# Three delays in a chunk clock: when the feed-forward transposes, the recurrence's gates and the last head group's attention are issued

## The chip, the cores and the metric

The kernel runs on one core of one Trainium2 chip. The metric is the time of one execution on the device in microseconds, as the median of several runs. A core has a matrix engine (PE, whose weight loads the profile lists apart as PEld), a vector engine (DVE), an activation engine (ACT), GpSimd (POOL) and a sync engine (SP); each has an instruction queue of its own and works it off in order. Here SP issues nearly all loads from HBM.

## The reference

Two transformer blocks over 256 tokens of width 2048, in float32. The first has a gated linear recurrence and a windowed attention side by side, then a feed-forward layer; the second has gated linear attention with decay, then a feed-forward layer.

```python
u = causal_depthwise_conv(u, conv_w[l], conv_b[l])
r = sigmoid(einsum(uh, wa) + ba); i = sigmoid(einsum(uh, wx) + bx)      # the recurrence's gates
...                                                                     # a linear scan over tokens
y_attn = sliding_window_attention(q, k, v, sinks[l])                    # 16 heads, 4 key/value heads
merged = gate_lru * (y_lru @ w_lru_out[l]) + gate_attn * (y_attn @ w_attn_out[l])
x = x + g1 * (merged @ w_o[l])
gate, up = jnp.split(h2 @ w_ffn_in[l], 2, axis=-1)
x = x + g2 * ((jax.nn.silu(gate) * up) @ w_ffn_out[l])                  # hidden width 5632
...                                                                     # the second block ends alike:
x = x + swiglu(rms_norm_2(x, norm_g[i, 1]), ffn_w_gu[i], ffn_w_down[i])
```

## The kernel before

**Chunks.** All large products run over *chunks*: a block of 512x512 weights, 1 MB, loaded by SP into a buffer `raw` (three of them). `split` casts each half of a chunk to a rounded part `hi` on ACT (line 173) and takes the remainder `lo` on DVE (line 175); there are three `hi` and three `lo` half-chunk buffers. `accumulate` then issues three matmuls per product (high by high, high by low, low by high): 48 matmuls of 256 columns per chunk, called narrow here (lines 197, 199, 201), or, where the output has tokens on partitions, 24 of 512 columns, called wide (lines 190 to 192). `project` runs the four chunks of one group of 512 output columns into two PSUM banks (of eight).

**The chunk clock.** Everything else is written as Python generators that are interleaved with the chunks. `spawn(gen, delay)` notes a generator that is due `delay` ticks later; `pump()` adds one tick and advances each generator that is due by one step, up to its next `yield n`, which makes it due again `n` ticks later; `finish` runs one to its end at once. There is a pump after every chunk. The pump also issues `steps`: slices of a matrix-vector product, each a 512 KB load `mvw` on SP's queue and one DVE operation `mva` that adds it up (line 247).

**The scheduler.** The program written in that order is then put in its final order by a list scheduler, which moves instructions between neighbouring pieces of work and gives the weight loads, `hi` and `lo` a head start (priority offset 2000). So the place in the chunk clock decides roughly, not exactly, where an instruction stands in its engine's queue.

**The three generators.** `turned` (line 657) transposes one feed-forward group: `sg`, the product of `silu(gate)` and `up` with tokens on partitions (DVE, line 724 in the first block, 969 in the second), goes through eight 128x128 transposes on PE (`tps`, line 666) into two banks; ACT copies each to `hid` (line 668) and DVE takes the remainder (line 669). `swiglu` runs it for 6 and then 5 groups in each block, 22 in all; the `fops` products that follow read `hid`. `recur` (line 558) does the recurrence of 512 channels in steps: convolution (`uc`), the eight gate matmuls `rps` (lines 578, 579), sigmoids and exponentials, a square root, the scan. `attend` (line 366) does four heads that share one key/value head in five steps: scores of two heads; scores of the other two, maximum and exponentials; sums and normalisation; two ticks later twelve transposes `tp` (line 405) with ACT copies to `p` (line 406); one tick later the products with the values `o` (lines 410 to 413) and the output pair `ya`. The `aops` products read `ya` of head group c in chunk c, and call `finish(attn[c])` before it.

Of the kernel before, what the change touches and what calls it, by code (L numbers as in the profile page):

```python
# [49 lines left out]
def block_pair_kernel(ctx: ExitStack, tc: tile.TileContext, a: dict):  # L50
# [78 lines left out]
    def spawn(gen, delay=0):  # L129
        task = [clock[0] + delay, gen]  # L130
        tasks.append(task)
        return task
# [46 lines left out]
    def accumulate(ps, ap, src, first, last, tokens=False):  # L179

        parts = split(ap, tokens)
        for kk in range(4):
            hi, lo = parts[kk // 2]
            wk = kk % 2
            fst, lst = first and kk == 0, last and kk == 3
            if tokens:
                for t in range(2):
                    tsl = slice(t * P, (t + 1) * P)
                    xh, xl = src.hi(kk)[:, tsl], src.lo(kk)[:, tsl]
                    nc.tensor.matmul(ps[t], xh, hi[:, wk, :], start=fst, stop=False)  # L190
                    nc.tensor.matmul(ps[t], xh, lo[:, wk, :], start=False, stop=False)  # L191
                    nc.tensor.matmul(ps[t], xl, hi[:, wk, :], start=False, stop=lst)  # L192
                continue
            for f in range(4):
                wsl = slice(f * P, (f + 1) * P)
                o = ps[f // 2][:, f % 2, :]
                nc.tensor.matmul(o, hi[:, wk, wsl], src.hi(kk), start=fst and f % 2 == 0,  # L197
                                 stop=False, skip_group_check=True)
                nc.tensor.matmul(o, hi[:, wk, wsl], src.lo(kk), start=False, stop=False,  # L199
                                 skip_group_check=True)  # L200
                nc.tensor.matmul(o, lo[:, wk, wsl], src.hi(kk), start=False, stop=lst,  # L201
                                 skip_group_check=True)

    def banks(name, tokens=False):
        return [bank(name, [P, 512] if tokens else [P, 2, T]) for _ in range(2)]
# [59 lines left out]
    def ada_steps(strip, queue=nc.gpsimd):  # L265


        def done(ps):
            if strip < 4:
                cols = ((16 + 4 * strip, 0, 4), (4 * strip, 4, 4))  # L270
            else:
                cols = ((8 * strip, 0, 8),)
            for j, p, n in cols:
                nc.vector.tensor_tensor(mod[:, j:j + n], ps[:, p:p + n], v("ada_b", j, n), ALU.add)

        return matvec([a["ada_w"][strip, k] for k in range(NK)], lambda k: cact[:, k:k + 1],
                      1024, done, queue)
# [183 lines left out]
    early = {}  # L461
    ga = {}
    attn = []
    for q in range(NG):
        ahead = ada_steps(q + 1) if q < NG - 1 else []
        count = sum(len(ks) for _, ks in plan[q])
        share = -(-len(ahead) // (count - 1))
        for g, ks in plan[q]:
            tok = g == 13
            if g in held:  # L470
                if q == 0:
                    early[g] = banks(f"e{g}", tok)
                ps = early[g]
            else:
                ps = banks("part")
            for k in ks:
                if g in held:
                    accumulate(ps, a["w_in"][g, k], h[k], k == 0, k == NG - 1, tok)
                else:
                    accumulate(ps, a["w_in"][g, k], h[k], k == ks[0], k == ks[-1])  # L480
                for st in ahead[:share]:
                    st()
                if ahead and len(ahead) <= share:
                    next_h()
                ahead = ahead[share:]
                lead[0] = PREP
                if q == NG - 1 and k < ks[-1]:
                    pump()
            if g not in held:
                fresh = g not in early  # L490
                if fresh:
                    early[g] = slot(f"e{g}")
                for b, part in enumerate(halves(early[g])):
                    if fresh:
                        nc.scalar.activation(part, ps[b], AF.Copy)
                    else:
                        nc.vector.tensor_tensor(part, ps[b], part, ALU.add)
                ps = halves(early[g])
            if q == NG - 1:
                if g == 12:  # L500
                    kv["k"] = evac_bias(ps, "kT", 48)
                elif g == 13:
                    kv["v"] = slot("vn", shape=[P, 2, 512])
                    for t in range(2):
                        nc.vector.tensor_tensor(kv["v"][:, t, :], ps[t], bv, ALU.add)
                elif g < 12:
                    attn.append(spawn(attend(g - 8, early[g]), 1 + 2 * (g - 8)))
                else:
                    ga[g - 18] = evac_bias(ps, "ga", 72 + 4 * (g - 18), AF.Sigmoid,
                                           early[g])  # L510
                pump()
# [46 lines left out]
    def recur(g, ups):  # L558
        lw = slot("lw", shape=[P, 4, 2, P])
        nc.sync.dma_start(lw, a["lru_w"][g])  # L560
        u = evac_bias(ups, "u", 4 * g)
        uc = slot("uc")
        for i in range(4):
            j = 4 * g + i
            nc.scalar.activation(uc[:, i, :], u[:, i, :], AF.Identity, bias=v("conv_b", j),
                                 scale=v("conv_w", 48 + j))
            for k in (2, 1, 0):
                s = 3 - k
                nc.vector.scalar_tensor_tensor(uc[:, i, s:], u[:, i, 0:T - s],
                                               v("conv_w", 16 * k + j), uc[:, i, s:],  # L570
                                               ALU.mult, ALU.add)
        yield 1
        r = slot("r")
        ig = slot("ig")
        for i in range(4):
            j = 4 * g + i
            ps = bank("rps", [P, 2, T])
            nc.tensor.matmul(ps[:, 0, :], lw[:, i, 0, :], uc[:, i, :], start=True, stop=True)
            nc.tensor.matmul(ps[:, 1, :], lw[:, i, 1, :], uc[:, i, :], start=True, stop=True)
            nc.scalar.activation(r[:, i, :], ps[:, 0, :], AF.Sigmoid, bias=v("lru_ba", j))  # L580
            nc.scalar.activation(ig[:, i, :], ps[:, 1, :], AF.Sigmoid, bias=v("lru_bx", j))
        yield 1
        nc.vector.tensor_tensor(ig, ig, uc, ALU.mult)
        av = slot("av")
        for i in range(4):
            j = 4 * g + i
            nc.scalar.activation(av[:, i, :], r[:, i, :], AF.Exp, scale=c8[:, j:j + 1])
            nc.scalar.activation(r[:, i, :], r[:, i, :], AF.Tanh, scale=nc8[:, j:j + 1])

        aa = slot("aa")  # L590
        nc.scalar.activation(aa, av, AF.Square)
        yield 1
        nc.vector.scalar_tensor_tensor(r, aa, 1.0, r, ALU.add, ALU.mult)
        nc.scalar.activation(r, r, AF.Sqrt)
        yield 1
        nc.vector.tensor_tensor(ig, ig, r, ALU.mult)
        for i in range(4):
            nc.vector.tensor_tensor_scan(r[:, i, :], av[:, i, :], ig[:, i, :], 0.0,
                                         ALU.mult, ALU.add)
        while g not in gelu:  # L600
            yield 1
        ge = gelu.pop(g)
        nc.vector.tensor_tensor(ge, ge, r, ALU.mult)
        y_lru[g] = split_act(ge, "yr")
# [66 lines left out]
    def swiglu(w_in, w_out, gate, up, update):  # L671
        for n, half in enumerate((range(0, 6), range(6, FG))):
            hid, turns = [], []
            for j in half:
                sg = gate(j)
                pump()
                gen = turned(up(sg, j))
                hid.append(next(gen))
                turns.append(spawn(gen, 1))
                pump()  # L680
            for f in range(NG):
                chunks = chunks_of(w_out, f, list(half))
                ps = banks("fops")
                for c in range(len(chunks)):
                    finish(turns[c])
                    accumulate(ps, chunks[c], hid[c], c == 0, c == len(chunks) - 1)
                    if c < len(chunks) - 1:
                        pump()
                update(n, f, ps)
                pump()  # L690
# [383 lines left out]
```

## Time and profile before

| | |
|---|---|
| runs | median 2764.09 us of 3 (2761.22 to 2767.21) |
| the profiled execution | 2761.13 us, of which the span of its instructions is 2759.4 us |
| PE busy, weight loads busy | 98% and 90% of the span |
| DVE, ACT, POOL busy | 65%, 48%, 1% |
| moved by DMA | 602 MB, 218 GB/s on average |
| mean granted PE clock | 0.997 |

In order of time from the span's start: the front with the first norm and partial projections (to 225 us), these with attention in between (to 317), the `aops` products (to 400), the recurrence with its projections (to 640), gates and merge (to 880), feed-forward layer one (880 to 1620), linear attention (to 2050), feed-forward layer two (to the end).

A timeline row reads: start in us, busy us, engine, line and operation, output<-inputs, size, and in brackets the idle time before it with what ended it. PE is pipelined and its ends are modelled, so a row's busy time is longer than the distance to the next start; distances between starts tell what PE lost. A row of the waits reads: who waited for whom: us in total, times, longest. A row of the windows gives per engine the busy us and instructions in the stretch, then the granted PE clock (PEclk), the DMA share and GB/s.

### The profile page before, as it was taken

What the parts mean: (1) busy time and instruction counts of PE and PEld (TensorE: products, weight loads), DVE (VectorE), ACT (ScalarE), POOL (GpSimd) and SP (SyncE); (2) the same over time, 40 slices, a digit from 0 to 9 for tenths busy, and PEclk for the clock granted to TensorE, in tenths of its full rate; (3) what the DMA queues carried; (4) which work ended last, traced back from release to release, by engine and by line L of the source; (5) the groups of instructions that cost most, each with busy time, mean ns of one, the idle gap of its engine ahead of it and who ended that gap; (6) DMA issues with size and microseconds to landing.
All of it is one profiled execution on the core that took longest, in us unless ns stands there. A gap on an engine that the chain in (4) does not pass through costs nothing.

```text
span 2759.4 us, 43921 instructions
## 1 busy us (share of the span) xinstructions
PE 2691.7 (98%) x18612; PEld 2478.1 (90%) x18612; DVE 1783.9 (65%) x2000; ACT 1321.7 (48%) x1531; POOL 25.7 (1%) x52
## 2 busy tenths in 40 slices
PE   4999999999999999999999999999999999999999
PEld 4999899999999788899888999899988889988899
DVE  8888866878887865444545677866654544444544
ACT  3446537874455444434444555555554443344443
POOL 1100000000000000000000000000000000000000
PEclk9999999999999999999999999999999999999999
DMA  9984785769985876555555544445555555555554
GB/s 357 365 306 153 248 325 190 262 236 339 341 289 184 290 248 216 183 197 187 188 191 183 199 163 169 151 142 180 192 190 183 184 195 186 199 183 192 187 195 161
DMA packets 100165, 602.00 MB, mean 218 GB/s; under 512 B 11120, under 2 KB 11632, under 8 KB 40576
## 3 DMA queue, kind: packets, MB, share of 16 engines
q1 hardware_dynamic: 93056, 574.03, 59.7%
q0 software_dynamic: 6912, 25.17, 2.4%
q8 instruction: 145, 2.38, 0.3%
q14 instruction: 52, 0.43, 0.0%
HBM read 597.06 MB, written 2.10 MB: 217 GB/s over the span
## 4 chain that ended last, share of the span: by engine, by line
PE 88%; DVE 5%; DMA 3%; issue 3%; ACT 1%; POOL 0%; SPq 0%; DVEq 0%; POOLq 0%; ACTq 0%
PE fgps L191 6%; PE fgps L190 6%; PE fgps L192 6%; PE fops L197 6%; PE fops L201 6%; PE fops L199 6%; PE fups L192 5%; PE fups L190 5%; PE fups L191 5%; DMA mvw<-ada_w 3%; DVE lo L175 2%; PE part L199 1%; PE part L197 1%; PE part L201 1%; ACT hi L173 1%
## 5 line engine op out<-in xcount | busy, mean ns | idle before, releaser
L175 DVE TENSOR_TENSOR lo<-raw,hi 128x1024 fp32r<-128x1024 f32 x928 | 1134.4, 1223 | 871.2 <-ACT hi L173 869.2
L173 ACT ACTIVATE hi<-raw 128x1024 fp32r<-128x1024 f32 x928 | 983.1, 1060 | 1263.2 <-PE fups L192 274.5
L197 PE MATMUL fops<-hid,hi 128*128 128x256 f32 x1408 | 389.0, 276 | 0.0
L201 PE MATMUL fops<-hid,lo 128*128 128x256 f32 x1408 | 388.9, 276 | 0.0
L199 PE MATMUL fops<-hid,hi 128*128 128x256 f32 x1408 | 388.8, 276 | 0.0
L190 PE MATMUL fups<-hi,h 128*128 128x512 f32 x704 | 274.0, 389 | 0.0
L191 PE MATMUL fups<-lo,h 128*128 128x512 f32 x704 | 273.9, 389 | 0.0
L192 PE MATMUL fups<-hi,h 128*128 128x512 f32 x704 | 273.9, 389 | 0.0
L190 PE MATMUL fgps<-hi,h 128*128 128x512 f32 x672 | 264.7, 394 | 0.0
L199 PEld LDWEIGHTS fops<-hid,hi 128*128 128x128 f32 x1408 | 264.3, 188 | 0.0
L201 PEld LDWEIGHTS fops<-hid,lo 128*128 128x128 f32 x1408 | 264.3, 188 | 0.0
L197 PEld LDWEIGHTS fops<-hid,hi 128*128 128x128 f32 x1408 | 264.3, 188 | 0.0
L192 PE MATMUL fgps<-hi,h 128*128 128x512 f32 x672 | 263.1, 391 | 0.0
L191 PE MATMUL fgps<-lo,h 128*128 128x512 f32 x672 | 262.2, 390 | 0.0
L247 DVE SCALAR_TENSOR_TENSOR mva<-mvw,cact,mva 128x1024 f32<-128x1024 f32 x180 | 230.5, 1280 | 32.3 <-DMA mvw<-ada_w 30.4
L190 PEld LDWEIGHTS fups<-hi,h 128*128 128x128 f32 x704 | 132.1, 188 | 27.5
L192 PEld LDWEIGHTS fups<-hi,h 128*128 128x128 f32 x704 | 132.1, 188 | 27.5
L191 PEld LDWEIGHTS fups<-lo,h 128*128 128x128 f32 x704 | 132.1, 188 | 27.3
L192 PEld LDWEIGHTS fgps<-hi,h 128*128 128x128 f32 x672 | 126.3, 188 | 26.0
L191 PEld LDWEIGHTS fgps<-lo,h 128*128 128x128 f32 x672 | 126.5, 188 | 25.4
L190 PEld LDWEIGHTS fgps<-hi,h 128*128 128x128 f32 x672 | 126.5, 188 | 25.0
L197 PE MATMUL part<-h,hi 128*128 128x256 f32 x512 | 145.4, 284 | 0.0
(322 smaller groups left out, 5424.0 us busy)
## 6 DMA issues: line engine op xcount, KB each, us to landing
raw<-w_in SPq DMA_DIRECT2D x88, 1024.0 KB, 5.3
raw<-w_ffn_in SPq DMA_DIRECT2D x88, 1024.0 KB, 4.8
raw<-ffn_w_gu SPq DMA_DIRECT2D x88, 1024.0 KB, 4.8
mvw<-ada_w SPq DMA_DIRECT2D x144, 512.0 KB, 7.1
raw<-gla_w_in SPq DMA_DIRECT2D x48, 1024.0 KB, 4.8
raw<-w_ffn_out SPq DMA_DIRECT2D x44, 1024.0 KB, 4.8
raw<-ffn_w_down SPq DMA_DIRECT2D x44, 1024.0 KB, 4.9
mvw<-ada_w POOLq DMA_DIRECT2D x48, 512.0 KB, 8.5
```

What stands on the lines that cost most here:

```text
L173: nc.scalar.activation(hi, rb, AF.Copy)
L175: nc.vector.tensor_tensor(lo, rb, f32(hi), ALU.subtract)
L190: nc.tensor.matmul(ps[t], xh, hi[:, wk, :], start=fst, stop=False)
L191: nc.tensor.matmul(ps[t], xh, lo[:, wk, :], start=False, stop=False)
L192: nc.tensor.matmul(ps[t], xl, hi[:, wk, :], start=False, stop=lst)
L197: nc.tensor.matmul(o, hi[:, wk, wsl], src.hi(kk), start=fst and f % 2 == 0, stop=False, skip_group_check=True)
L199: nc.tensor.matmul(o, hi[:, wk, wsl], src.lo(kk), start=False, stop=False, skip_group_check=True)
L201: nc.tensor.matmul(o, lo[:, wk, wsl], src.hi(kk), start=False, stop=lst, skip_group_check=True)
L247: nc.vector.scalar_tensor_tensor(state["acc"], w, col(k), state["acc"], ALU.mult, ALU.add)
```

## The change

Three delays become other numbers. The transposes of a feed-forward group become due two ticks after their group instead of one. The recurrence waits two ticks between convolution and gates instead of one. The fourth head group's attention starts five ticks after it is spawned instead of seven. No instruction's work is changed.

```diff
-                    attn.append(spawn(attend(g - 8, early[g]), 1 + 2 * (g - 8)))
+                    attn.append(spawn(attend(g - 8, early[g]), (1, 3, 5, 5)[g - 8]))
...
         # in recur(), between the convolution and the gates
-        yield 1
+        yield 2
...
         # in swiglu(), after up(sg, j)
-                turns.append(spawn(gen, 1))
+                turns.append(spawn(gen, 2))
```

What that does to the queues is seen at three places. First, PE at the end of a feed-forward group (`fups` is the up product of the group, `fgps` the gate product of the next). Before:

```order
L192 MATMUL fups<-hi,h 128x512
L666 MATMUL tps<-ident,sg 128x128 x2
L190 MATMUL fgps<-hi,h 128x512
L191 MATMUL fgps<-lo,h 128x512
L666 MATMUL tps<-ident,sg 128x128 x6
L192 MATMUL fgps<-hi,h 128x512
```

And now, where between the two products 24 matmuls of the next group's first chunk stand ahead of the transposes (its first and last rows are shown):

```order
L192 MATMUL fups<-hi,h 128x512
L190 MATMUL fgps<-hi,h 128x512
...
L192 MATMUL fgps<-hi,h 128x512
L666 MATMUL tps<-ident,sg 128x128 x8
L190 MATMUL fgps<-hi,h 128x512
```

The transposes moved from both sides of the group's end to one place a chunk later, eight in a row. On ACT the copies `hid` then stand behind ten weight casts after the second `silu` instead of eight, and on DVE the remainders behind three `lo` after `sg` instead of one. At the end of a half's last group the chunk ahead of them is the first of `fops`.

Second, PE from the second head group's value products to the fourth's (`sps` are scores; s_2564 is the third head group's, s_2922 and s_2778 are the fourth's, `part` the last projections). Before:

```order
L413 MATMUL o_2749<-p_2637,vn 128x512
...
L405 MATMUL tp<-ident,s_2564 128x128 x4
L405 MATMUL tp<-ident,s_2565 128x128 x8
L368 MATMUL sps<-kT,e_632 128x128
...
L410 MATMUL o_2994<-p_2898,vn 128x512
...
L197 MATMUL aops<-ya,hi 128x256
...
L405 MATMUL tp<-ident,s_2922 128x128 x4
L405 MATMUL tp<-ident,s_2923 128x128 x6
L410 MATMUL o_3315<-p_3234,vn 128x512
L405 MATMUL tp<-ident,s_2923 128x128 x2
```

And now:

```order
L413 MATMUL o_2749<-p_2637,vn 128x512
L368 MATMUL sps<-kT,e_632 128x128
...
L405 MATMUL tp<-ident,s_2564 128x128 x4
...
L410 MATMUL o_3033<-p_2941,vn 128x512
...
L405 MATMUL tp<-ident,s_2778 128x128 x4
L405 MATMUL tp<-ident,s_2779 128x128 x8
L197 MATMUL aops<-ya,hi 128x256
...
L410 MATMUL o_3192<-p_3112,vn 128x512
```

The fourth group's first scores moved ahead of the third's transposes; its transposes moved from behind three chunks of `aops` (144 matmuls) to ahead of the first, with its value products 48 matmuls after them instead of among them. The third group's value products now stand 86 matmuls after its transposes instead of 48. On SP, five chunks of `w_attn_out` stand ahead of the next `mvw` loads where there were three, and on DVE the first `mva` of that stage stands behind all of the fourth group's softmax instead of within it. POOL's queue is the same.

Third, PE in the recurrence, within the first `gps` product. Before:

```order
L201 MATMUL gps<-h,lo 128x256
L578 MATMUL rps<-uc,lw 128x256
L579 MATMUL rps<-uc,lw 128x256
...
L199 MATMUL gps<-h,hi 128x256
L578 MATMUL rps<-uc,lw 128x256
L579 MATMUL rps<-uc,lw 128x256
...
L201 MATMUL gps<-h,lo 128x256
```

The four pairs of gate matmuls stood two and two, some ten matmuls apart, after the first chunk. Now all eight stand in one row after the second chunk:

```order
L201 MATMUL gps<-h,lo 128x256
L578 MATMUL rps<-uc,lw 128x256
L579 MATMUL rps<-uc,lw 128x256
...
L579 MATMUL rps<-uc,lw 128x256
L197 MATMUL gps<-h,hi 128x256
```

ACT's queue now holds 41 loads of activation tables where it held 47: the sigmoids of a recurrence group are no longer cut in two by its exponentials.

## The prediction

> **What bounds the kernel now.** I read the page first, then the waits, then PE's timeline at the places that the change moves.
>
> ```profile
> span 2759.4 us, 43921 instructions
> PE 2691.7 (98%) x18612; PEld 2478.1 (90%) x18612; DVE 1783.9 (65%) x2000; ACT 1321.7 (48%) x1531; POOL 25.7 (1%) x52
> PE 88%; DVE 5%; DMA 3%; issue 3%; ACT 1%; POOL 0%; SPq 0%; DVEq 0%; POOLq 0%; ACTq 0%
> ```
>
> PE is busy 98% of the span and has 88% of the chain that ends last. No instruction leaves PE by this change, so all it can return is time in which PE stands still, plus time in which PE runs slowly because it stood still. The span less PE's busy time is 68 us, most of it in the front, which isn't touched. The transposes appear among PE's waits:
>
> ```profile
> PE tps L666 <- DVE sg L724: 5.0, 11, 1.9
> PE tps L666 <- DVE sg L969: 3.9, 11, 0.4
> ```
>
> Read: 11 groups in each block, 22 in all, and at each PE waits for the DVE product that the transposes read. Since ends are modelled, these rows understate it, and I count starts instead.
>
> **The feed-forward transposes.** One group's end in the first block:
>
> ```profile
> 1097.14 0.39 PE L192 MATMUL fups<-hi,h 128*128 128x512 f32 x1
> 1097.82 0.44 PE L666 MATMUL tps<-ident,sg 128*128 128x128 f32 x2 [0.29 <-DVE sg L724]
> ...
> 1098.33 0.40 PE L191 MATMUL fgps<-lo,h 128*128 128x512 f32 x1
> 1098.56 0.82 PE L666 MATMUL tps<-ident,sg 128*128 128x128 f32 x6
> 1099.14 0.47 PE L192 MATMUL fgps<-hi,h 128*128 128x512 f32 x1
> 1099.45 0.39 PE L190 MATMUL fgps<-hi,h 128*128 128x512 f32 x1
> ```
>
> An undisturbed wide matmul takes 0.23 us (1098.33 to 1098.56). Six transposes with one wide matmul behind them take 0.89 (1098.56 to 1099.45), so a transpose is 0.11 with the change-over in it. The stretch from 1097.14 to 1099.45 holds four wide matmuls and eight transposes: 4 x 0.23 + 8 x 0.11 = 1.80 of 2.31 us. Lost: 0.51. The transposes now come 24 wide matmuls or 5.5 us later, and the start that DVE's product held up, 0.68 us after the last matmul here and 2.28 at the worst group below, is long past. In the second block, and at that worst group:
>
> ```profile
> 2109.00 0.39 PE L192 MATMUL fups<-hi,h 128*128 128x512 f32 x1
> ...
> 2111.61 0.40 PE L191 MATMUL fgps<-lo,h 128*128 128x512 f32 x1
> ```
>
> ```profile
> 957.20 0.39 PE L192 MATMUL fups<-hi,h 128*128 128x512 f32 x1
> 959.48 0.64 PE L666 MATMUL tps<-ident,sg 128*128 128x128 f32 x2 [1.89 <-DVE sg L724]
> ...
> 962.91 0.43 PE L191 MATMUL fgps<-lo,h 128*128 128x512 f32 x1
> ```
>
> Both hold five wide matmuls and the eight transposes, 2.03 us: lost 0.58 and 3.68. Sum: ten groups of the first block at 0.51, one at 3.68, eleven of the second at 0.58: 5.1 + 3.7 + 6.4 = 15.2 us. Bounds: the waits that PE's own rows show, 5.0 + 3.9 = 8.9, are the least; 15.2 the most. I take 15.2, since starts don't depend on a modelled end.
>
> What would become late next is the weight preparation, as the `hid` copies and remainders now stand among other casts:
>
> ```profile
> 1099.09 1.09 ACT L668 ACTIVATE hid<-tps 128x512 fp32r<-128x512 f32 x2 [0.47 <-PE tps L666]
> 1099.80 1.28 DVE L669 TENSOR_TENSOR hid<-tps,hid 128x512 fp32r<-128x512 f32 x2
> 1104.45 1.06 ACT L173 ACTIVATE hi<-raw 128x1024 fp32r<-128x1024 f32 x1 [1.66 <-PE fgps L192]
> 1105.54 1.23 DVE L175 TENSOR_TENSOR lo<-raw,hi 128x1024 fp32r<-128x1024 f32 x1 [1.49 <-ACT hi L173]
> ```
>
> Per half chunk (12 matmuls, 2.7 us) ACT idles 1.66 and DVE 1.49; the transposes give 0.9 more. The pairs take 1.09 and 1.28, and with three buffers PE has up to two more prepared halves in hand. They fit, so I cost them at nothing; without that cover it would be 1.28 each time. `hid` is first read by `fops`, for the last group five chunks on. `sg` lives one chunk longer: 8 slots of `h2`, 12 of `hid`, two `sg` and one `mva` make 23 of the 24, and the two `tps` banks with four of gate and up products make six of eight.
>
> **The clock.** A pause also costs speed afterwards. PE's granted clock in the stretch behind the two longest pauses that the change removes:
>
> ```profile
> 321.40:324.90 3.50, 3.50 (x10) 2.06 (x10) 3.13 (x5) 0.68 (x2) 0.00 (x0) 0.53 0.98 358
> 960.00:963.00 3.00, 3.00 (x12) 2.51 (x12) 1.87 (x4) 1.19 (x2) 0.00 (x0) 0.50 0.84 319
> ```
>
> Half speed for some 3.4 us each loses 1.7 us, which stands already in the 3.68 above and in the next term. [...]
>
> **The last head group.** Its transposes and value products now:
>
> ```profile
> 317.25 0.28 PE L201 MATMUL aops<-ya,lo 128*128 128x256 f32 x1
> 319.43 0.63 PE L405 MATMUL tp<-ident,s 128*128 128x128 f32 x3 [1.90 <-DVE s L397]
> 321.06 1.81 PE L405 MATMUL tp<-ident,s 128*128 128x128 f32 x7 [1.00 <-DVE s L397]
> ...
> 328.39 0.28 PE L201 MATMUL aops<-ya,lo 128*128 128x256 f32 x1
> ```
>
> The same for the third group, undisturbed (eleven of twelve transposes, then the three value products):
>
> ```profile
> 283.73 1.36 PE L405 MATMUL tp<-ident,s 128*128 128x128 f32 x11
> 284.94 0.39 PE L368 MATMUL sps<-kT,e 128*128 128x128 f32 x2
> ...
> 291.70 1.02 PE L410 MATMUL o<-p,vn 128*128 128x512 f32 x2
> 294.27 0.38 PE L368 MATMUL sps<-kT,e 128*128 128x128 f32 x2
> ```
>
> Twelve transposes are 1.32 us (1.21 for eleven), the value products 2.57. From 317.25 to 328.39 there are these and eight narrow matmuls at 0.11: 4.8 of 11.1 us. Some 0.5 of change-overs remain, so 5.8 us can return. Not all will. The normalisation that PE waited for stood among `mva` operations on DVE; now it runs ahead of them. But the fourth group's exponentials now stand on ACT ahead of the third's copies `p`, and with them a table load:
>
> ```profile
> 303.13 1.28 ACT L385 ACT_TABLE_LOAD   x1
> ...
> 305.49 1.26 ACT L388 ACTIVATE s<-s,st 128x128 f32<-128x128 f32 x4
> ...
> 307.61 1.70 ACT L388 ACTIVATE s<-s,st 128x256 f32<-128x256 f32 x4
> ```
>
> That is 4.2 us of ACT ahead of the copies, against 38 narrow matmuls (4.3 us) that the third group's value products moved back: balanced, not safe. How long PE then waits at the two value products no row shows. Ends: nothing, as for the third group now; and 5.8, as long as the stall that goes. I take 2.8, half, since neither is nearer; the term is 5.8 - 2.8 = 3.0. No load is issued by `attend`. But the `mva` loads slide behind two more weight loads on SP, and behind the softmax on DVE, and in this stage they wait:
>
> ```profile
> 360.11 1.28 DVE L247 SCALAR_TENSOR_TENSOR mva<-mvw,cact,mva 128x1024 f32<-128x1024 f32 x1 [3.13 <-DMA mvw<-ada_w]
> 362.59 0.39 PE L201 MATMUL aops<-ya,lo 128*128 128x256 f32 x1 [1.92 <-DVE lo L175]
> ```
>
> A load that lands late blocks DVE, the weights' `lo` behind it come late, and PE stands. Such a wait may go or come again with the new order: between -1.9 and +1.9 us, and I take 0.
>
> **The gates.** In the four recurrence groups the second half of the gate matmuls comes late:
>
> ```profile
> 433.76 0.28 PE L199 MATMUL gps<-h,hi 128*128 128x256 f32 x1
> 434.35 0.67 PE L578 MATMUL rps<-uc,lw 128*128 128x256 f32 x2 [0.32 <-DVE uc L569]
> ...
> 528.28 0.28 PE L199 MATMUL gps<-h,hi 128*128 128x256 f32 x1
> 529.75 0.67 PE L578 MATMUL rps<-uc,lw 128*128 128x256 f32 x2 [1.20 <-ACT hi L173]
> ...
> 580.53 0.67 PE L578 MATMUL rps<-uc,lw 128*128 128x256 f32 x2 [0.32 <-DVE uc L569]
> ```
>
> The distances are 0.59 and 1.47 where 0.11 would do: 0.48 lost in the first group (the second and fourth read alike) and 1.36 in the third, 2.8 in all. A chunk later the convolution is done, and one of two returns from gates to projection goes in each group (0.1 from 1099.14 to 1099.45 against 0.23, so 0.4 in all), 3.2 at most. Least is 0: eight sigmoids then come to ACT at once, between the casts. I take 2.8, with the six fewer table loads on ACT in its favour. The scan ends one chunk later, after the first of the four `glps` chunks for the last group, and its result is needed behind all four: that costs nothing. The load of `lw` stays in the first step.
>
> **Sum.** 15.2 + 3.0 + 2.8 + 0 = 21.0 us. On the profiled execution, 2761.1 us (the span and 1.7 around it), that gives 2740.1. The median of the runs, 2764.1, stands 3.0 above it, and so I predict 2743 us, 0.76% faster. A measurement of this kernel can tell about 0.2%, 5.5 us, from no change.
>
> **Rivals.**
>
> *The two smaller terms come to nothing.* The feed-forward part works, but in the attention and the recurrence new waits eat what the old ones return. For it: PE waits there for one DVE operation among many in a list order that no one row fixes. Against: both places have undisturbed twins in the rows above. Then 2764.1 - 15.2 = 2748.9.
>
> [...]
>
> *The wait at the transposes is a fixed change-over* between kinds of matmul, and moves along. Then the ordinary 11.5 us stay, and 2743 + 11.5 = 2754.5. Against: at 1098.56 the change-over to transposes costs nothing (0.23 after a wide matmul).
>
> *Slower: the weight preparation slips.* If ACT's and DVE's slack is gone where `hid` now stands, each group pays up to 1.28 us on PE. The point at which it decides is where the cost of a group passes the 0.51 to 0.58 gained, plus the 5.8 us of the other terms over 22 groups, so about 0.8 us; with the 5.5 us of the bound, 1.1. At 1.28 it is 22 x 1.28 - 21.0 = 7.2 slower: 2771. For it: both engines work in order and a late cast stops PE. Against: the slack of 1.66 and 1.49 above, of which no more is asked than is there, except where `mva` (1.28 us apiece) shares DVE, in the first groups of the first block.
>
> **How the numbers follow.** The forecast 0.60; smaller terms nothing 0.16; clock drops stay 0.08; fixed change-over 0.06; fixed change-over and smaller terms nothing together, which leaves the 3.7 us of one group, 2760.4, 0.06; slower 0.04. Faster by over 0.2% are the first four, 0.90; within 0.2% the fifth, 0.06; slower 0.04. The range: low, all three terms at their most (15.2 + 5.8 + 3.2 + 1.9 = 26.1): 2738.0, less two for the spread of the runs (2761 to 2767), 2736. High: only the least of the first term, 8.9: 2755, which takes in the first four cases.
>
> **What would show it.** In the new profile: no wait of `tps` for `sg`, and 1.8 us for four wide matmuls and the eight transposes at each group; the granted clock at full through both places; twelve `tp` of the fourth group in one row of 1.3 us; the first `rps` 0.1 to 0.3 us behind its neighbour. Wrong it would be if PE waited for `lo` behind the `hid` pairs, or if `o` of the third or fourth group waited for `p` for more than 3 us.

## The result and the profile after

| | before | after |
|---|---|---|
| median of the runs | 2764.27 us of 4 (2761.22 to 2767.21) | 2733.84 us of 4 (2732.10 to 2738.96) |
| the profiled execution | 2761.13 us | 2733.50 us |
| mean granted PE clock | 0.997 | 0.999 |

The ratio is 0.9896 (95% interval 0.9883 to 0.9910): 1.0% faster, where 0.76% was forecast. The time lies 2.2 us under the low end of the predicted range. A second comparison, on another chip, gave 0.9909 (0.9893 to 0.9925), 2735.95 against 2763.65 us. All ratios here and below leave out the one disturbed run, of the kernel with the feed-forward delay alone, which took 9582.05 us at a mean granted clock of 0.438.

The page of the changed kernel, in the lines shown of before:

```profile
span 2731.7 us, 43911 instructions
PE 2680.5 (98%) x18612; PEld 2479.3 (91%) x18612; DVE 1782.3 (65%) x2000; ACT 1310.7 (48%) x1525; POOL 25.7 (1%) x52
PE 95%; DVE 2%; issue 1%; DMA 1%; ACT 1%; SPq 0%; DVEq 0%; ACTq 0%
```

PE's share of the chain rose from 88% to 95%; DVE's fell from 5% to 2%, DMA's from 3% to 1%. PE's busy time fell by 11 us with the same 18612 matmuls, as rows that hold a stall or run at half clock read longer (before, seven transposes in the stall read 1.81 us, eleven undisturbed ones 1.36). Neither row of `tps` for `sg` is left among the waits.

PE's timeline at the end of a feed-forward group:

```profile
1085.02 0.39 PE L190 MATMUL fgps<-hi,h 128*128 128x512 f32 x1
1085.24 0.39 PE L191 MATMUL fgps<-lo,h 128*128 128x512 f32 x1
1085.47 0.39 PE L192 MATMUL fgps<-hi,h 128*128 128x512 f32 x1
1085.70 1.03 PE L666 MATMUL tps<-ident,sg 128*128 128x128 f32 x8
1086.49 0.48 PE L190 MATMUL fgps<-hi,h 128*128 128x512 f32 x1
1086.80 0.39 PE L191 MATMUL fgps<-lo,h 128*128 128x512 f32 x1
```

Four wide matmuls and the eight transposes take 1.78 us, from 1085.02 to 1086.80, against 2.31 before and the 1.80 that was to be seen.

The last head group's transposes, and the value products of the third and the fourth group:

```profile
298.38 0.28 PE L199 MATMUL part<-h,hi 128*128 128x256 f32 x1
299.23 1.13 PE L410 MATMUL o<-p,vn 128*128 128x512 f32 x2 [0.58 <-ACT p L406]
...
303.07 1.48 PE L405 MATMUL tp<-ident,s 128*128 128x128 f32 x12
304.30 0.37 PE L197 MATMUL aops<-ya,hi 128*128 128x256 f32 x1
...
309.74 0.28 PE L201 MATMUL aops<-ya,lo 128*128 128x256 f32 x1
309.86 1.02 PE L410 MATMUL o<-p,vn 128*128 128x512 f32 x2
```

Twelve `tp` stand in one row of 1.23 us without a wait, and the fourth group's `o` start 0.12 us behind their neighbour. The new wait that was feared came at the third group's `o`: 0.85 us between starts where 0.11 would do, 0.74 us lost.

The windows at the two places where the clock was at half (the second one of 20 us, since what stood at 960 before now runs some 12 us earlier):

```profile
311.00:314.50 3.50, 3.50 (x22) 2.64 (x21) 3.47 (x6) 1.34 (x4) 0.00 (x0) 1.00 0.77 282
940.00:960.00 20.00, 20.00 (x94) 16.65 (x93) 11.39 (x12) 8.45 (x10) 0.00 (x0) 1.00 0.81 294
```

The granted clock is 1.00 in both. And the gates of the third recurrence group:

```profile
524.33 0.28 PE L201 MATMUL gps<-h,lo 128*128 128x256 f32 x1
524.45 0.59 PE L578 MATMUL rps<-uc,lw 128*128 128x256 f32 x2
524.88 0.59 PE L579 MATMUL rps<-uc,lw 128*128 128x256 f32 x2
...
527.47 0.59 PE L579 MATMUL rps<-uc,lw 128*128 128x256 f32 x2
527.71 0.47 PE L197 MATMUL gps<-h,hi 128*128 128x256 f32 x1
```

The first follows after 0.12 us, and none waits.

**Where the 27.6 us between the two profiled executions went.** The distances between the first matmuls of two products give the span by stretches, in us. (In the kernel before the `aops` products begin at 301.05 us and not at 317, where the stall stands, so the whole `aops` stage is in the second stretch.)

| stretch | before | after | difference | forecast |
|---|---|---|---|---|
| start to first scores | 213.3 | 214.5 | +1.2 | 0 |
| first scores to recurrence (attention, `aops`) | 190.0 | 181.3 | -8.7 | -3.0 |
| recurrence (`ups` to `glps`) | 194.1 | 190.2 | -3.9 | -2.8 |
| gates, merge, `w_o` | 270.0 | 269.9 | -0.1 | 0 |
| feed-forward one | 742.4 | 733.1 | -9.2 | -8.8 |
| linear attention | 409.6 | 409.6 | 0.0 | 0 |
| feed-forward two | 739.9 | 733.2 | -6.7 | -6.4 |

The feed-forward terms came as forecast. The attention's is nearly three times its forecast. How much of such a stretch is the order and how much is one execution, the experiments tell.

### The profile page after: what moved, and what is told of

The parts are those of the page before. It is cut to its first block, busy times and chain, and to the rows that moved or that the text cites. A ratio compares the mean times of both kernels' runs of the same rounds, so it can differ in the third digit from the quotient of the medians.

```text
span 2731.7 us, 43911 instructions
## 1 busy us (share of the span) xinstructions
PE 2680.5 (98%) x18612; PEld 2479.3 (91%) x18612; DVE 1782.3 (65%) x2000; ACT 1310.7 (48%) x1525; POOL 25.7 (1%) x52
## 4 chain that ended last, share of the span: by engine, by line
PE 95%; DVE 2%; issue 1%; DMA 1%; ACT 1%; SPq 0%; DVEq 0%; ACTq 0%
PE fgps L192 6%; PE fgps L191 6%; PE fgps L190 6%; PE fops L197 6%; PE fups L190 6%; PE fups L192 6%; PE fups L191 6%; PE fops L201 6%; PE fops L199 6%; PE part L197 2%; PE part L199 2%; PE part L201 2%; PE lops L201 1%; PE ups L197 1%; PE wops L197 1%; PE ups L201 1%
## 5 line engine op out<-in xcount | busy, mean ns | idle before, releaser
L247 DVE SCALAR_TENSOR_TENSOR mva<-mvw,cact,mva 128x1024 f32<-128x1024 f32 x180 | 230.6, 1281 | 26.6 <-DMA mvw<-ada_w 24.5
```

The source lines that it names most:

```text
L247: nc.vector.scalar_tensor_tensor(state["acc"], w, col(k), state["acc"], ALU.mult, ALU.add)
```

## Experiments

Below, "us by the ratio" is the ratio's distance from 1 times 2764 us.

**Each part alone** (three runs on one chip). First only the feed-forward delay:

```diff
-                turns.append(spawn(gen, 1))
+                turns.append(spawn(gen, 2))
```

> Only the feed-forward transposes come two ticks after their group; the other two delays as before. If the three delays act each on its own place, the two feed-forward layers alone get shorter, by what the full change shows there: 9.2 us in the first and 6.7 in the second, about 2748 us where before is 2764. If they help each other (the attention's new place shifts the loads and with them the one group with the 2 us wait), the first layer keeps 3 us or more of its loss and the whole stands at 2751 or above.

Measured: 0.9961 (0.9947 to 0.9975), 10.8 us by the ratio. In the trace both feed-forward layers have the lengths of the changed kernel, 733.1 and 733.2 us. Other stretches are longer than in the kernel before, though nothing ahead of the feed-forward layer differs: the recurrence has 195.6 instead of 194.1.

Then only the attention:

```diff
-                    attn.append(spawn(attend(g - 8, early[g]), 1 + 2 * (g - 8)))
+                    attn.append(spawn(attend(g - 8, early[g]), (1, 3, 5, 5)[g - 8]))
```

> Only the fourth head group's attention starts two ticks earlier. Each on its own place: from the first scores to the end of the w_attn_out products 8.7 us shorter, the rest of the span unchanged within 0.5 us, about 2755.5 us. Helping each other: the stretch gains 5.8 at most, as the prediction bounded the stall there, or later stretches move by over 1 us.

Measured: 0.9976 (0.9965 to 0.9987), 6.6 us by the ratio. First scores to recurrence: 184.5 us, 5.5 less than before. Its order is that of the changed kernel, and the stall is gone in the same way; but here three waits of `aops` for `lo` are left, where the changed kernel had none. By its number this is the expectation's second case, but it is no sign of help between the parts: up to the first `ups` every engine has the same operations in the same order in both kernels, so the 3.2 us between 184.5 and 181.3, nearly all of them the three waits, are a difference between two executions of one order. The waits of that stage in this trace:

```profile
DVE mva L247 <- DMA mvw<-ada_w: 15.3, 9, 4.2
PE aops L201 <- DVE lo L175: 2.3, 3, 1.3
```

Then only the recurrence:

```diff
-        yield 1
+        yield 2
```

> Only the gates of the recurrence come two ticks after the convolution. Each on its own place: the recurrence's stretch 3.9 us shorter and the rest unchanged, about 2760 us. Helping each other: 2.8 or less here, as the four late starts in the profile of before alone would give.

Measured: 0.9986 (0.9974 to 0.9998), 3.9 us by the ratio; the recurrence's stretch is 190.2 us, the same as in the changed kernel.

**The slices out of the way, the attention where it was.**

```diff
-    credit[1] = 1.1
+    credit[0], credit[1] = -5.0, 1.1
```

> As before, with the attention where it was, but the slices of the matrix-vector product (512 KB load, one DVE operation each) start about five ticks later in the w_attn_out stage, so that neither DVE's queue nor SP's holds them amid the last softmax. If the last head group's stall and the two waits for lo come from these slices, the stretch from the first scores to the end of the w_attn_out products gets at least 6 us shorter without any move of the attention. If they come from the place of the attention right ahead of its use, at least 4 of the 5.8 us of stall stay. The slices left over are issued at once ahead of the w_o products, which can cost some us there; that stretch is read apart.

Measured: 1.0048 (1.0033 to 1.0063), slower. But first scores to recurrence fell to 179.1 us, 10.9 less than before (some 1.8 of it because a reduction of 16 matmuls moved to a later stretch), and the stall is gone with the attention's start at seven ticks; no `aops` waits for `lo` either. The loss came later: the recurrence, where slices now stand at other places, took 5.7 us more than before, and the slices that were left over are run at once ahead of `w_o`, and PE stands for them.

```profile
783.13 3.57 PE L259 MATMUL mvp<-ones,mva 128*128 128x1 f32 x16 [13.66 <-DVE mva L247]
```

So the stall was made by the slices on DVE amid the fourth group's softmax. The rows show it, first before, then after, then with the slices out of the way (`L397` is the normalisation that the transposes wait for, `L245` and `L247` are slices):

```profile
294.48 0.75 DVE L245 TENSOR_SCALAR mva<-mvw,cact 128x1024 f32<-128x1024 f32 x1
...
315.41 1.28 DVE L247 SCALAR_TENSOR_TENSOR mva<-mvw,cact,mva 128x1024 f32<-128x1024 f32 x1
317.85 1.23 DVE L247 SCALAR_TENSOR_TENSOR mva<-mvw,cact,mva 128x1024 f32<-128x1024 f32 x1
319.00 0.67 DVE L397 TENSOR_SCALAR s<-s,st 128x128 f32<-128x128 f32 x3
```

```profile
298.03 0.87 DVE L397 TENSOR_SCALAR s<-s,st 128x256 f32<-128x256 f32 x3
312.51 0.74 DVE L245 TENSOR_SCALAR mva<-mvw,cact 128x1024 f32<-128x1024 f32 x1
```

```profile
305.56 0.68 DVE L397 TENSOR_SCALAR s<-s,st 128x128 f32<-128x128 f32 x3
309.37 1.47 PE L405 MATMUL tp<-ident,s 128*128 128x128 f32 x12
318.81 0.74 DVE L245 TENSOR_SCALAR mva<-mvw,cact 128x1024 f32<-128x1024 f32 x1
```

Before, eight slices stand from 294.48 to the normalisation at 319.00. In that stretch none of them waits for its load, so it is their own time on DVE, 0.75 and seven times some 1.28 us, and not a late load that pushes the normalisation back. After, the first slice comes 14 us behind the normalisation's end. With the slices out of the way the normalisation begins at 305.56, and the twelve transposes stand in one row without a wait.

**The whole again, without the attention, and half of its step** (one chip). The changed kernel a second time:

> The changed kernel once more, beside the kernel before and beside the version without the attention's new place. The three parts timed alone gave 10.8, 6.6 and 3.9 us of 2764, together 21.3; the whole gave 30.4 on another chip and against few runs. Theory A (the parts add up, the rest was scatter of the first 220 us and of the loads): about 22 to 24 us faster than the kernel before, ratio 0.992 to 0.9915, and the stretch from the first scores to the recurrence, 190.0 us before, is 183 to 185 us this time, with waits of PE for lo back among the aops products. Theory B (the parts help each other): again 28 us or more, ratio 0.990 or less, and that stretch again near 181.

Measured: 0.9909 (0.9893 to 0.9925), 25.2 us by the ratio, 27.7 by the medians. Its trace has 181.35 us from first scores to recurrence and no wait for `lo` there, as B had it. The time lies between the two theories, whose intervals it doesn't part.

The attention's delay put back in the changed kernel:

```diff
-                    attn.append(spawn(attend(g - 8, early[g]), (1, 3, 5, 5)[g - 8]))
+                    attn.append(spawn(attend(g - 8, early[g]), 1 + 2 * (g - 8)))
```

> The two other delays as in the changed kernel, the last head group's attention back at seven ticks. Against the changed kernel this is the worth of the attention's place with the other two in. Theory A: 5 to 7 us slower than the changed kernel, 15 to 17 us faster than the kernel before (ratio 0.994), the stall of 4 to 6 us at the fourth group's transposes and value products is back, clock drop included. Theory B: 9 us or more slower than the changed kernel.

Measured: 0.9922 (0.9908 to 0.9936), 2741.43 us, 5.5 above the changed kernel by the medians. That is near what the attention gave alone (6.6) and speaks for A. By the two traces the attention's stretch differs by more, 8.1 us (189.48 against 181.35), since the changed kernel's second run had no wait for `lo` there. So help of one part for another isn't seen, and not excluded by these times either. Stall and clock drop are back, the drop 6.8 us long this time:

```profile
322.42 0.28 PE L201 MATMUL aops<-ya,lo 128*128 128x256 f32 x1
324.59 0.78 PE L405 MATMUL tp<-ident,s 128*128 128x128 f32 x3 [1.90 <-DVE s L397]
```

```profile
324.60:331.40 6.80, 5.47 (x15) 3.23 (x16) 5.12 (x11) 1.96 (x4) 0.00 (x0) 0.52 0.93 347
```

The changed kernel with the last head group at six ticks:

```diff
-                    attn.append(spawn(attend(g - 8, early[g]), (1, 3, 5, 5)[g - 8]))
+                    attn.append(spawn(attend(g - 8, early[g]), (1, 3, 5, 6)[g - 8]))
```

> The changed kernel with the last head group's attention started six ticks after it is spawned instead of five (seven before). If only what stands around the softmax on DVE decides (the first mva operations of the stage come at the third chunk of aops), the transposes of the fourth group still stand ahead of those and the time is the same as the changed kernel's within 2 us. If the place on PE decides, part of the stall is back: 2 to 4 us slower than the changed kernel, with PE waiting at tp for the normalisation.

Measured: 2736.28 us, ratio 0.9908 (0.9895 to 0.9922): the changed kernel's time. The twelve transposes stand one chunk into `aops`, in one row and without a wait, since the normalisation at 301.39 is again ahead of the first slice at 309.05.

```profile
306.56 0.28 PE L201 MATMUL aops<-ya,lo 128*128 128x256 f32 x1
306.68 1.47 PE L405 MATMUL tp<-ident,s 128*128 128x128 f32 x12
307.91 0.37 PE L197 MATMUL aops<-ya,hi 128*128 128x256 f32 x1
```

**Two more delays on top.**

```diff
-                    attn.append(spawn(attend(g - 8, early[g]), (1, 3, 5, 5)[g - 8]))
+                    attn.append(spawn(attend(g - 8, early[g]), (2, 3, 5, 5)[g - 8]))
...
         # in decays(), after the logarithm
-            yield 1
+            yield 2
```

> The changed kernel with two more delays: the first head group's attention starts two ticks after it is spawned instead of one (PE stands 1.59 us at the first scores, which wait for kT), and the decays wait two ticks between their logarithm and the subtraction instead of one (DVE stands 4.10 us at that subtraction for ACT, the weights' lo behind it come late and PE stands 1.11, 0.60 and 1.11 us in gkps/gqps). If these waits go as those of the change went, 1.6 + 2.8 = 4.4 us less than the changed kernel, ratio 0.998. Rival: the first group's transposes and value products collide with the second's scores, as all four groups stand closer, and the subtraction blocks DVE at another place: no gain or 1 to 2 us slower.

Measured: 0.9900 (0.9887 to 0.9914), 2734.43 us against 2735.95: not to be told apart. The wait at the first scores is gone, and the waits in linear attention shrank from 2.8 to 1.3 us with 0.45 of new ones; but in the profiled execution one slice landed late in the recurrence, which took 193.20 us with every engine's order as in the changed kernel, and cost PE 2.6 us at an `ups` product. That shows what size the scatter has against such steps.

```profile
544.71 1.28 DVE L247 SCALAR_TENSOR_TENSOR mva<-mvw,cact,mva 128x1024 f32<-128x1024 f32 x1 [2.33 <-DMA mvw<-ada_w]
```

**The feed-forward delay again, and three ticks** (one chip). Again `spawn(gen, 2)` alone:

> The feed-forward delay alone, a second time. Its stretches of the trace gave 16.0 us less, its timed runs 10.8 (ratio 0.9961, 0.9947 to 0.9975). Everything ahead of the feed-forward layer is the same program as in the kernel before. Theory: the 5 us between the two are the scatter of the loads ahead of the feed-forward layer, and a second time, on another chip, the ratio comes out at 0.9942 (16.0 us), within 0.9930 to 0.9955. Rival: something of the change costs time ahead of or between the stretches, and the ratio stays at 0.996.

Measured: 0.9949 (0.9935 to 0.9963), 14.1 us by the ratio. The interval holds both 0.9942 and, just, 0.9961, so neither is excluded; the two feed-forward layers are again 733.1 and 733.2 us.

```diff
-                turns.append(spawn(gen, 1))
+                turns.append(spawn(gen, 3))
```

> The kernel before with the feed-forward transposes due three ticks after their group instead of one (two in the change). If the 22 waits are waits for the DVE product alone, which one tick of 5.5 us more than covers, a third tick gives nothing more: the same four stretches as with two, 15.9 to 16.1 us under the kernel before in the trace. If the place among the weights' casts matters as well, the stretches differ from those with two ticks by more than 1 us, and above all the last group of a half, whose copies are then a tick closer to the products that read them, would show a wait of fops for hid.

Measured: 0.9942 (0.9929 to 0.9955), 16.0 us by the ratio; the layers have 733.0 and 733.2 us, and `fops` never waits for `hid`. One tick more covered the DVE product, a second one more gave nothing.

**The slices begun earlier**, on top of the changed kernel:

```diff
     for q in range(NG):
+        if q == NG - 1:
+            for strip in (4, 5, 8, 9, 6, 7):
+                steps += ada_steps(strip, nc.sync)
+            credit[1] = 0.4
...
-    for strip in (4, 5, 8, 9, 6, 7):
-        steps += ada_steps(strip, nc.sync)
-    credit[1] = 1.1
+    credit[1] = 0.8
```

> The changed kernel with the slices of the matrix-vector product begun one stage earlier, during the attention (0.4 a tick), where the DMA share is 0.43, and fewer of them among the aops products (0.8 a tick instead of 1.1), where it is 0.84. If the waits for lo in the aops stage and the recurrence come from loads of slices that land late on a busy memory, they get rarer and the median falls by 1 to 3 us below the changed kernel's (ratio 0.989 to the kernel before). Rival: a slice on DVE amid the softmax of the first three head groups brings back for them the stall that the fourth group lost, and the attention's stretch (89.84 us in the changed kernel) grows by 3 us or more: slower than the changed kernel.

Measured: 0.9912 (0.9898 to 0.9926): no gain over the changed kernel. The attention's stretch to the first `aops` is 89.84 us, the same, so the rival's 3 us didn't come either; a wait of 1.29 us for `lo` is still among the `aops`.

**The recurrence without slices.** Why the recurrence gave more than forecast is seen at the third group. The trace of the second run with the feed-forward delay alone, DVE and then PE:

```profile
530.18 1.28 DVE L247 SCALAR_TENSOR_TENSOR mva<-mvw,cact,mva 128x1024 f32<-128x1024 f32 x1 [2.89 <-DMA mvw<-ada_w]
531.38 1.22 DVE L175 TENSOR_TENSOR lo<-raw,hi 128x1024 fp32r<-128x1024 f32 x1
532.52 1.66 DVE L569 SCALAR_TENSOR_TENSOR uc<-u,vec,uc 128x255 f32<-128x255 f32 x4
```

```profile
532.07 0.28 PE L199 MATMUL gps<-h,hi 128*128 128x256 f32 x1
535.81 0.67 PE L578 MATMUL rps<-uc,lw 128*128 128x256 f32 x2 [3.46 <-issue]
```

DVE stands 2.89 us for the load of one slice, the convolution `uc` behind it is late, and PE loses 3.63 (3.74 between starts). In the trace of before the same slice waited only this long:

```profile
524.12 1.28 DVE L247 SCALAR_TENSOR_TENSOR mva<-mvw,cact,mva 128x1024 f32<-128x1024 f32 x1 [0.63 <-DMA mvw<-ada_w]
```

The kernel before, with no slice during the recurrence:

```diff
-    credit[1] = 1.0
+    credit[1] = 0.0
     rec = []
```

> The kernel before with no slice of the matrix-vector product issued during the recurrence; all that are left are then forced ahead of w_o, which costs a long stop there, so that only the recurrence's stretch is to be read. In five traces of the old order PE lost at the third group's gates 0.73 us more than DVE had waited at the one slice before the convolution (0.63 and 1.36, 1.50 and 2.23, 1.71 and 2.44, 2.06 and 2.79, 2.89 and 3.63). Theory: the late load is the cause. Without slices each of the four groups loses the ordinary 0.5 us, and the stretch is 190.2 + 1.9 = 192 us, within 0.7. Rival: the place of the gates alone costs it, and the third group still loses 1.3 us or more: 193.5 us or above.

Measured: the stretch is 191.5 us, and the four groups lose 0.48 or 0.49 us each, the third like the others:

```profile
526.20 0.28 PE L199 MATMUL gps<-h,hi 128*128 128x256 f32 x1
526.79 0.67 PE L578 MATMUL rps<-uc,lw 128*128 128x256 f32 x2 [0.32 <-DVE uc L569]
```

So the slice ahead of the convolution is the cause of what the third group loses beyond 0.5 us; that it is the lateness of its load is told by the five traces, in which the loss grows by as much as the wait. The stretch by itself does not tell the theory from the rival: 16 matmuls of a reduction, 1.8 us, moved out of it with the slices, and with them it would be 193.3 (190.2, the 1.9 of the four late starts, and some 1.1 for the changes between gate and projection matmuls in the old order come to as much). (The run as a whole, a single one, took 2807.1 us, for the slices forced later. Half of the slices among the `aops` are missing in it as well.)

**All traces together.** The stretches by the delay that was in force, leaving out kernels that moved the slices or other waits of that stretch (three ticks count as the new delay for the feed-forward layers), in us:

| stretch | old delay: mean (least to most, traces) | new delay | difference | forecast |
|---|---|---|---|---|
| attention and `aops` | 189.5 (188.3 to 190.3, 6) | 182.4 (181.3 to 184.5, 3) | -7.1 | -3.0 |
| recurrence | 195.6 (194.1 to 197.9, 5) | 190.7 (190.2 to 193.2, 6) | -4.9 | -2.8 |
| feed-forward one | 741.4 (740.0 to 742.6, 5) | 733.1 (733.0 to 733.1, 9) | -8.3 | -8.8 |
| feed-forward two | 739.7 (739.5 to 739.9, 5) | 733.2 (733.2 to 733.2, 9) | -6.5 | -6.4 |

Together 26.8 us, which agrees with both timings of the whole (28.7 and 25.2 by the ratios).

## Why the prediction was wrong, point by point

*The feed-forward transposes: right.* Forecast 15.2, measured 15.9 in the one pair of traces and 14.8 between the means. The waits were waits for DVE's product, one tick covers them, and the casts had the room: no matmul of the feed-forward layers waits for `lo` behind the `hid` pairs. That the term fitted so closely is in part luck: the 3.68 us of the worst group were one sample too. In the five traces of the old delay there the distance between the starts at that group's first transpose was 1.61 to 2.87 us (2.28 in the trace that was read), DVE waited there for slices (1.57 us at 949.29 in that trace), and in the same trace the clock fell behind it (0.50 over 960.00 to 963.00).

*The last head group and the `aops` stage: the mechanism right, the terms mis-sized.* The step that failed is the halving: 2.8 of 5.8 us was given away for new waits at the value products "since neither is nearer". What came was 0.74 us at one `o`, so the lower end, nothing, was the nearer one. The second half is the `aops` stage, costed between -1.9 and +1.9 and taken at 0. In the profiled pair two waits for `lo`, 2.8 us between starts, went. Whether that is the new order's doing stays open: the old order had one or two such waits in each of six traces, the new one none, none and three, and where slices were missing from that stage there were none in the old order either. So the 8.7 us of the profiled pair are 2.8 from these waits, less the 0.7 of the new wait, and 6.6 from the stall, which was put at 5.8. Between the means it is 7.1, by the timed runs 5.5 to 6.6, against 3.0. What the stall hung on was told too loosely: not the place of the transposes decides but whether DVE normalises ahead of the stage's first slice. Six ticks do as well as five, and the old place does without slices.

*The gates: right in kind, the bound too low.* The profiled pair gave 3.9, above the 3.2 called the most; the means give 4.9. In the pair the four late starts gave the 2.8 that was forecast, and the changes between gate and projection matmuls some 1.1 us by the distances between starts, where 0.4 was put. Beyond the pair, the third group's 1.36 us was read as a constant. It is 0.73 us and the time by which one slice lands late, 0.63 in that trace and 1.50 to 2.89 in four others. In the new order the convolution is a chunk ahead, and no trace shows a wait at the gates; five traces of the stretch agree within 0.1 us. In the sixth a late slice cost 2.6 us at another reader, so the stretch isn't free of such waits.

*From the profiled execution to the median.* 3.0 us were added as if they lay in untouched work. In part they lay in the waits that the change removes: that execution's recurrence was 1.5 us shorter than the mean of the five in the old order. Another 1.7 us lay in its front, 213.3 against a mean of 215.0 in twelve traces of the same front. The changed kernel's profiled execution stands only 0.3 under its median.

*The range* was built from one trace's waits as the most that could return, 26.1 us taken off the median. Waits that depend on a load have no most in one trace: the one at the third group's convolution read 0.63 us in that trace and 2.89 in another. By the medians 30.4 us returned in the first comparison and 27.7 in the second; the second, taken off the same median, would have ended within the range, so by how little it was missed is chance. That the three terms together were put at 21.0 is not.

*The rivals.* "The two smaller terms come to nothing": no, the attention alone gives 6.6 us and the recurrence alone 3.9, both intervals clear of 1. "The clock drops stay": no, the windows above read 1.00. No run shows the 3.4 us that this case adds to the forecast (2746.4). The drop at the last head group (0.53 over 321.40 to 324.90, behind a pause of 2.2 us between starts) went with its stall and returned with it where the delay was put back (0.52 over 324.60 to 331.40, again behind a pause of 2.2 us); the drop at the worst group (0.50 over 960.00 to 963.00, behind 2.3 us) went with its wait. "A fixed change-over": no, the 22 waits of 0.5 us are gone. "Slower, the weight preparation slips": no wait of that kind appeared.

*Named signs.* All of them came, which speaks for the mechanism and not for the sizes: no wait of `tps`, 1.78 us, full clock at both places, one row of `tp`, `rps` 0.12 us behind its neighbour, no wait of `o` above 3 us.

## What to carry to other kernels

On an engine that works in order, an operation that waits for a load delays whatever stands behind it (above, 2.89 us of DVE at one slice cost PE 3.63), so put short work that another engine waits for ahead of such operations, or a tick further from its reader. When sizing a wait that hangs on a load, one trace gives a sample and not a bound: read the same place in several executions, and count what the change makes independent of the load as gained on average, not as in that trace. Moving one reader away does not protect the others: another operation behind a late load can still stand (2.6 us at an `ups` product above). And before an offset between a profiled execution and the median is carried over unchanged, ask whether it lies in the very waits that the change removes.

## What the runs showed of the hardware that was not expected

The granted clock fell behind pauses of 1.6 and 2.5 us, to 0.51, and stayed at 1.00 behind pauses of 2.1 and 2.6. The windows behind these pauses, in that order (pauses between starts, beyond a matmul's own time), of the kernel before, the second run of the changed kernel, the kernel before again, and the kernel with two more delays:

```profile
82.30:85.70 3.40, 3.40 (x18) 3.40 (x18) 2.62 (x7) 0.51 (x1) 0.00 (x0) 0.51 1.01 406
```

```profile
83.40:90.20 6.80, 6.80 (x34) 6.80 (x34) 3.82 (x10) 0.51 (x1) 0.00 (x0) 0.51 0.94 383
```

```profile
362.60:366.60 4.00, 4.00 (x35) 4.00 (x36) 4.00 (x4) 1.06 (x1) 0.00 (x0) 1.00 0.62 201
```

```profile
547.00:551.00 4.00, 3.81 (x33) 3.81 (x34) 4.00 (x5) 1.06 (x1) 0.00 (x0) 1.00 0.46 131
```

The first drop lasted 3.4 us and the second 6.8; at the stop of 13.7 us ahead of `w_o`, with the slices out of the way, the clock was at 0.51 for 17.1 us (772.60 to 789.70; the stop ends at 783.13). What sets the pauses ahead of a drop apart from the others was not tested. And the first 215 us, the same program throughout, took from 210.7 to 221.8 us in twelve traces, with a DMA share of 0.89 to 0.91 in its first 200 us in the four traces where it was read; those 11.1 us are nearly as much as the 13.3 by which 20 timed runs of the kernel before differ on one chip (2754.41 to 2767.66).
